# Output stage of a tiled pooling trunk: the inner form of product P2 from the second block on, with its weight sums made in place

## The chip, the cores and the metric

The kernel runs on one core of a Trainium2 chip. The metric is the device time of one execution in microseconds (us). It was run three times: 909.86, 910.41 and 911.19 us, median 910.41 us. One further execution was profiled; every view named below is of that one.

## What is computed

The layer is one pre-norm residual sub-layer and a final norm, over 4096 frames of 1024 channels, all in float32:

```python
u, gate = jnp.split(h @ in_w, 2, axis=-1)
pooled = jnp.stack([trailing_mean(ug[:, :, g], w) for g, w in enumerate((2, 4, 8, 16))], axis=2) - ug
mixed = jnp.einsum('bsgc,gcd->bsgd', pooled, group_w) + group_b
y = mixed.reshape(b, s, 1024) * scale * jax.nn.silu(gate)
out = rms_norm(x + y @ out_w, final_norm_w)
```

Here `h` is the normed input. The change is in the last line, the product `y @ out_w` with the residual and the final norm behind it, which is called the output stage below.

## The kernel before, in words

**Stages.** The kernel first forms weights, then multiplies the normed input by two halves of the widened projection (steps "a" and "b", four blocks of 1024 frames each), pools, and stores `y` to DRAM as `yd`. The output stage (steps "o") then takes eight blocks of 512 frames, numbered 0 to 7. Every step is one product of a seven-product Strassen-Winograd scheme, so each block of the output stage has seven steps, in the order P1, P7, P6, P2, P5, P4, P3 (`ORDER_OUT`).

**One product.** A block's `y` (512 frames x 1024 channels) is split in four quarters of 256 frames x 512 channels, `out_w` in four quarters of 512 x 512. Each product multiplies a sum of quarters of `y` by a sum of quarters of `out_w`. Every float32 operand is split into a high part (a copy on ScalarE, which rounds it) and a remainder (a subtraction on VectorE); `split` (line 167 and around) does this. A product of two split operands takes three passes: high by high, high by remainder, remainder by high (`mm3`, line 603). The split operand of `y` lies in one of four tiles `op0` to `op3`, taken in turn, and is TensorE's stationary operand in this stage; the split weights lie in tiles `w1` to `w7`, one pair for each product, for the whole stage. A plain product is two row groups x four k-tiles x three passes = 24 matmuls of 128 x 512.

**The inner form.** From block 2 on, P2 is not done plainly. Its own operands (256 x 512 by 512 x 512) are split in quarters again and multiplied by seven smaller products: 7 x two k-tiles x three passes = 42 matmuls of 128 x 256 (`product_inner`, line 701). Five of them are issued in the step of P2, one inside P5 and one behind it. `split_inner` makes four sums of the `y` operand's quarters (128 x 256 each, on VectorE) and splits the operand and the sums, so the step takes two op tiles. Three of the seven inner weights are quarters of the split weight tile `w2`, read as they are. The other four (P7, P6, P5, P4) are sums of quarters of the raw weight, `wod2` in DRAM. `form_inner` makes them once, in block 1: `load_inner` loads the two raw halves, stage 0 makes the four sums in two fresh tiles, stages 1 and 2 split two sums each into four tiles kept for the rest of the run (`kept`, tiles named `inner`).

**Tiles.** All else shares 19 tiles of 128 x 1024 floats: `st0` to `st10` and `vt0` to `vt7`. `take` pops the tile that has been free longest from one of two lists; `give` puts one back when the program text is done with it. The reuse is by program order: an instruction that writes a tile taken again waits until whatever used it last, a store's reading included, is over.

**Order.** `advance` loads four steps ahead and, in the output stage, splits two steps ahead (`split_reach`), so in the step of block 0's P3 the operand of block 1's P7 is formed and split. A scheduler then fixes one order of instructions for each engine. Engines run their own list in that order and wait for each other by semaphores.

**Behind a product.** `evict_o` moves the results from the PSUM banks: P1 to the banks of the sum on ScalarE, P7, P6 and P2 to residual rows `hs` on ScalarE, with `x` added by a GpSimd-issued transfer (`add_h`, line 884), P5, P4 and P3 by additions on VectorE (line 1067). After P4 and after P3, `finish` squares the 256 rows on ScalarE (line 943), takes the root, has four tiny GpSimd operations sharpen the reciprocal, scales the rows on VectorE (line 947), stores them to `out` (line 951) and gives their tiles back.

Of the kernel before, what the change touches and what calls it, by code (L numbers as in the profile page):

```python
# [10 lines left out]
F32 = mybir.dt.float32  # L11
F32R = mybir.dt.float32r
# [3 lines left out]
P = 128  # L16
D = 1024
S = 4096
H = 512
# [11 lines left out]
P1, P2, P3, P4, P5, P6, P7 = range(1, 8)  # L31
# [33 lines left out]
def kernel(  # L65
# [38 lines left out]
    mem = ctx.enter_context(tc.tile_pool(name="mem", bufs=1))  # L104
# [6 lines left out]
    def new_w(i):  # L111
        return [
            mem.tile([P, 2, 2, H], F32R, tag=f"w{i}_{h}", name=f"w{i}_{h}") for h in range(2)
        ]

    w = {i: new_w(i) for i in (P1, P2, P6, P7)}
    ops = [mem.tile([P, 4 * H], F32R, tag=f"op{i}", name=f"op{i}") for i in range(4)]
    sts = [mem.tile([P, D], F32, tag=f"st{i}", name=f"st{i}") for i in range(NS)]
    st = Slots(sts)

    def renew(t):
        i = next(i for i, u in enumerate(sts) if u is t)
        return mem.tile([P, D], F32R, tag=f"st{i}", name=f"inner{i}")

    st.renew = renew
    vt = Slots(
        [mem.tile([P, 2 * (HIST + H)], F32, tag=f"vt{i}", name=f"vt{i}") for i in range(NV)]
    )
# [11 lines left out]
    keep = [3]  # L140

    def take(pattern="p (a b) -> p a b", pool=None, **sizes):
        sizes = sizes or {"a": 2}
        if pool is None:
            spare = len(vt.free) > keep[0] or not st.free
            pool = vt if spare and vt.age() < st.age() else st
        return pool.take(lambda t: t[:, 0:D].rearrange(pattern, **sizes))
# [4 lines left out]
    def give(ap):  # L152
        next(p for p in (st, vt, early, early5) if id(ap) in p.used).give(ap)

    def add(dst, a, b):
        nc.vector.tensor_tensor(out=dst, in0=a, in1=b, op=ALU.add)  # L156

    def sub(dst, a, b):
        return nc.vector.tensor_tensor(out=dst, in0=a, in1=b, op=ALU.subtract)  # L159
# [4 lines left out]
    def copy(dst, src, func=AF.Copy):  # L164
        return nc.scalar.activation(dst, src, func)  # L165

    def split(dst, src):

        latest_copy[0] = copy(dst[:, 0], src).ins
        latest_split[0] = sub(dst[:, 1], src, dst[:, 0].bitcast(F32)).ins  # L170
# [104 lines left out]
    parts, t2 = {}, {}  # L275
# [157 lines left out]
    sums, held = {}, {}  # L433
# [25 lines left out]
    def store_rs(b, half, rs):  # L459
        nc.gpsimd.dma_start(out=rd[b][half][0].rearrange("(p j) -> p j", j=4), in_=rs)  # L460
# [41 lines left out]
    def next_op(pattern, **sizes):  # L502
        t = ops[turn[0] % 4]
        turn[0] += 1
        return t.rearrange(pattern, **sizes)
# [123 lines left out]

    inner, inner_w, kept = {}, {}, []

    def quarter(u, j):

        return u.rearrange("p k (s a) -> p k s a", s=2)[:, :, :, j * P : (j + 1) * P]

    def load_inner():
        inner_w["raw"] = [take() for _ in range(2)]
        for h, u in enumerate(inner_w["raw"]):  # L640
            nc.sync.dma_start(out=u, in_=wod[P2][h])

    def form_inner(stage):

        pattern, sizes = "p (n k s a) -> p n k s a", dict(n=2, k=2, s=2)
        if stage == 0:
            us = inner_w.pop("raw")
            b11, b12 = (quarter(us[0], j) for j in range(2))
            b21, b22 = (quarter(us[1], j) for j in range(2))
            raw = inner_w["sums"] = [take(pattern, **sizes) for _ in range(2)]  # L650
            (t3, t2), (t1, t4) = ([r[:, n] for n in range(2)] for r in raw)
            sub(t3, b22, b12)
            add(t2, t3, b11)
            sub(t1, b22, t2)
            sub(t4, b21, t2)
            for u in us:
                give(u)
            return
        r = inner_w["sums"][stage - 1]
        hi, lo = (kept.pop().rearrange(pattern, **sizes) for _ in range(2))  # L660
        copy(hi, r)
        sub(lo, r, hi.bitcast(F32))
        give(r)
        for n, i in enumerate(((P7, P6), (P5, P4))[stage - 1]):
            inner_w[i] = [v[:, n] for v in (hi, lo)]
        for i, (h, j) in {P1: (0, 0), P2: (1, 0), P3: (1, 1)}.items():
            inner_w[i] = [quarter(w[P2][h][:, s], j) for s in range(2)]

    def split_inner(u):

# [232 lines left out]

    def split_o(b, i):
        s = oxs[b]
        if i == P2 and b > 1:
            return split_inner(s["12"])
        t = next_op("p (s a b) -> p s a b", s=2, a=4)
        if i == P7:
            s["3"] = take("p (a b) -> p a b", a=4)  # L910
            sub(s["3"], s["11"], s["21"])
        elif i == P6:
            add(s["21"], s["21"], s["22"])
            sub(s["11"], s["21"], s["11"])
        elif i == P3:
            sub(s["12"], s["12"], s["11"])
            give(s.pop("11"))
        key = {P1: "11", P7: "3", P6: "11", P2: "12", P5: "21", P4: "22", P3: "12"}[i]
        split(t, s[key])
        if i not in (P1, P6, P2):  # L920
            give(s.pop(key))
        return t
# [329 lines left out]
    for n, (h, k) in enumerate(chunks):  # L1252
        o = fold(
            1, k, gw[1], ru[1, k], pairs_of[n], early5, n < 2, spread_first if n == 1 else None
        )
# [103 lines left out]
        )  # L1359

    scales, summed = {}, []
    stages = (P6, P5, P4)
    stages = (P6, P5, P4)

    for n in range(2, len(steps)):
        kind, b, i = steps[n]
        ahead = kind == "a" and b + 1 < NB
        keep[0] = 5 if kind == "b" and b == NB - 1 else 3
        advance("load", n, load, load_reach)
        if ahead:  # L1370
            rows, squares = row_plan(b)
            for half, rs in scales.items():
                store_rs(b + 1, half, rs)
                load_rstd(b + 1, half)
            scales.clear()
            for j in squares.get(i, ()):
                with tc.issue_after(latest_copy[0] if n == 3 else evicted[0]):
                    square_row(b + 1, j // 4, j % 4)
                if j % 4 == 3:
                    summed.append(j // 4)  # L1380
            for j in rows.get(i, ()):
                load_row(b + 1, j // 4, j % 4, early if b == 0 and i == P7 else None)
        if kind == "o" and b == 1 and len(kept) < 4 and not inner_w:
            while len(kept) < 4 and len(st.free) > 2:
                kept.append(st.keep())
            if len(kept) == 4:
                load_inner()
        elif kept:
            keep[0] = 0
        advance("split", n, split_step, split_reach)  # L1390
        if kind == "o" and b == 1 and i in stages:
            with tc.issue_after(latest_split[0]), tc.issue_after(latest_copy[0]):
                form_inner(stages.index(i))
        with tc.issue_after(latest_split[0]) if summed else nullcontext():
            for half in summed:
                scales[half] = stats(b + 1, half)
        summed.clear()
        if n == 2:
            with tc.issue_after(first_saves[0]):
                for place, u in stores:  # L1400
                    nc.gpsimd.dma_start(out=place, in_=u)
            for place, u in stores:
                if id(u) in early5.used:
                    give(u)
        with tc.issue_after(latest_split[0]):
            form(n + 2)
        if kind == "a" and b == 0:
            with tc.issue_after(latest_split[0]):
                rest_of_first(n)
        pool_due(n)  # L1410
        since = n - (NB - 1) * len(ORDER_IN) - 2
        if 0 <= since < len(ORDER_IN):
            form_wb(ORDER_IN[since])
        run(n)
        if kind == "a" and b == 2 and i == P7:
            save_t3()
        if 0 <= since < len(ORDER_IN):
            with tc.issue_after(evicted[0]):
                split_wb(ORDER_IN[since])
        if 0 <= since + 1 < len(ORDER_IN):  # L1420
            load_wb(ORDER_IN[since + 1])
        if kind in ("a", "b"):
            pool_later(n)
            if kind == "a":
                pool_due(n)
            if kind == "b" and b == NB - 1:
                load_w(wod, i)
            if kind == "b" and b in (1, 2) and i == P5:
                make_wo(b - 1)
            if kind == "b" and b == NB - 1 and i == P3:  # L1430
                f = take("p (a b) -> p a b", a=2)
                nc.sync.dma_start(
                    out=f.rearrange("p a b -> p (a b)"), in_=final_w.partition_broadcast(P)
                )
                fw.append(f)
# [52 lines left out]
```

## Time and profile before

| | us |
|---|---|
| median of 3 runs (lowest to highest) | 910.41 (909.86 to 911.19) |
| the profiled execution, whole | 910.49 |
| its span, first to last instruction | 908.7 |
| around the span | 1.79 |
| VectorE, ScalarE, GpSimd busy in the span | 715.5, 485.9, 84.6 |
| granted TensorE clock, mean | 0.999 |

The output stage fills the last third. TensorE's products of block 0 run from 614.87 to 651.13 us, those of block 1 from 651.13 to 687.39, and so on to block 7, behind whose products the last evictions and stores follow. Rows of the timeline give start, duration, engine, line, operation and tiles, and in brackets the idle time ahead with what ended it.

### The profile page before, as it was taken

The page shows a single profiled execution, that of the slowest core. Times are in us where ns is not written, and L with a number is a line of the kernel's source. Part 1 is how long each engine was busy: PE and PEld are TensorE (multiplying, and loading weights), DVE is VectorE, ACT ScalarE, POOL GpSimd, SP SyncE. Part 2 cuts the span into 40 slices and gives each one's busy share as a digit, 9 for nine tenths or more (in the row PEclk, how much of TensorE's full clock was granted, in tenths as well). Part 3 has the DMA queues.
Part 4 walks back from the last instruction along what each step waited for, and adds up shares of the span by engine and source line. Part 5 has one row for each costly group of instructions (what it writes and reads, how often), then busy time and mean ns, then how long its engine had stood idle before and what let it go on. Part 6 is the DMA issues. An engine that isn't in the chain of part 4 may idle for free.

```text
span 908.7 us, 11590 instructions
## 1 busy us (share of the span) xinstructions
PE 900.7 (99%) x4320; PEld 790.1 (87%) x4320; DVE 715.5 (79%) x843; ACT 485.9 (53%) x735; POOL 84.6 (9%) x166
## 2 busy tenths in 40 slices
PE   9999999999999999999999999999999999999997
PEld 7888888888888888888888888888888898988886
DVE  3889995985995997685786599599759768868686
ACT  7869547447446555355345445645545535445444
POOL 0020100100110000000000000001122113212200
PEclk9999999999999999999999999999999999999999
DMA  9987776577575454134616715618585675675732
GB/s 343 401 300 230 268 241 240 190 267 245 218 271 193 162 207 140 47 140 138 255 72 217 267 70 174 200 54 225 179 234 160 169 205 162 163 220 156 180 139 94
DMA packets 70841, 178.10 MB, mean 196 GB/s; under 512 B 6528, under 2 KB 24320, under 8 KB 70784
## 3 DMA queue, kind: packets, MB, share of 16 engines
q1 hardware_dynamic: 58160, 144.82, 46.0%
q0 software_dynamic: 11904, 31.48, 13.3%
q10 hardware_dynamic: 720, 1.06, 0.3%
q8 instruction: 34, 0.56, 0.3%
q14 instruction: 23, 0.19, 0.1%
HBM read 116.50 MB, written 60.83 MB: 195 GB/s over the span
## 4 chain that ended last, share of the span: by engine, by line
PE 95%; DVE 2%; DMA 1%; ACT 1%; issue 0%; DVEq 0%; ACTq 0%; SPq 0%
PE bank L603 89%; PE bank L701 3%; PE bank L406 3%; DMA st<-wvd 1%; DMA t3d<-st 0%; DMA early<-in_group_w 0%; DVE vt L1067 0%; DVE st L159 0%; ACT st L974 0%; ACT st L446 0%; DVE vt L162 0%; PE bank L472 0%; DVE op L159 0%; DVE vt L1026 0%; DVE st L156 0%
## 5 line engine op out<-in xcount | busy, mean ns | idle before, releaser
L603 PE MATMUL bank<-op,w 128*128 128x512 f32 x2688 | 581.2, 379 | 0.2 <-ACT st L165 0.2
L603 PEld LDWEIGHTS bank<-op,w 128*128 128x128 f32 x2688 | 507.8, 189 | 72.9 <-ACT st L165 0.6
L603 PE MATMUL bank<-w,op 128*128 128x512 f32 (+1 forms) x1212 | 262.2, 377 | 0.0
L603 PEld LDWEIGHTS bank<-w,op 128*128 128x128 f32 x1212 | 226.0, 189 | 31.0
L159 DVE TENSOR_TENSOR op<-st,op 128x1024 fp32r<-128x1024 f32 x129 | 156.5, 1220 | 76.4 <-ACT op L165 76.0
L165 ACT ACTIVATE op<-st 128x1024 fp32r<-128x1024 f32 x129 | 134.7, 1052 | 123.3 <-PE bank L603 82.6
L165 ACT ACTIVATE vt<-bank 128x512 f32<-128x512 f32 x105 | 61.4, 593 | 44.7 <-PE bank L603 44.2
L159 DVE TENSOR_TENSOR op<-vt,op 128x1024 fp32r<-128x1024 f32 x43 | 52.4, 1220 | 20.8 <-ACT op L165 20.6
L165 ACT ACTIVATE op<-vt 128x1024 fp32r<-128x1024 f32 x43 | 45.0, 1052 | 28.9 <-PE bank L603 24.9
L165 ACT ACTIVATE st<-bank 128x512 f32<-128x512 f32 x67 | 39.0, 592 | 38.0 <-PE bank L603 26.1
L884 POOL DMA_DIRECT2D st<-in_x x19 | 16.9, 894 | 387.7 <-DVE op L159 354.1
L159 DVE TENSOR_TENSOR st<-st,st 128x1024 f32<-128x1024 f32 (+1 forms) x43 | 46.7, 1108 | 3.2 <-ACT st L943 1.3
L165 ACT ACTIVATE bank<-bank 128x512 f32<-128x512 f32 x48 | 27.9, 581 | 35.6 <-PE bank L603 35.4
L755 DVE TENSOR_TENSOR_SCAN vt<-vt,window 128x1040 f32<-128x1040 f32 x16 | 38.1, 2379 | 2.8 <-ACT vt L165 2.7
L159 DVE TENSOR_TENSOR w<-st,w 128x1024 fp32r<-128x1024 f32 x25 | 30.2, 1220 | 11.7 <-ACT w L165 11.7
L165 ACT ACTIVATE w<-st 128x1024 fp32r<-128x1024 f32 x25 | 26.0, 1052 | 16.3 <-PE bank L603 10.8
L806 DVE SCALAR_TENSOR_TENSOR st<-vt,colt,st 128x512 f32<-128x512 f32 x46 | 32.4, 746 | 1.7 <-ACT st L165 1.6
L165 ACT ACTIVATE st<-st 128x1024 f32<-128x1024 f32 x16 | 16.9, 1058 | 29.9 <-DVE st L156 29.7
L801 DVE SCALAR_TENSOR_TENSOR vt<-vt,vt 128x1024 f32<-128x1024 f32 x24 | 29.3, 1221 | 0.3
L947 DVE SCALAR_TENSOR_TENSOR vt<-vt,ors,st 128x1024 f32<-128x1024 f32 x18 | 22.5, 1282 | 8.0 <-POOL ors L225 8.0
L162 DVE TENSOR_TENSOR st<-st,vt 128x1024 f32<-128x1024 f32 x22 | 26.1, 1216 | 2.1 <-DMA vt<-rd 2.1
L1067 DVE TENSOR_TENSOR st<-bank,st 128x512 f32<-128x512 f32 x23 | 15.8, 689 | 13.8 <-PE bank L603 13.7
(136 smaller groups left out, 661.6 us busy)
## 6 DMA issues: line engine op xcount, KB each, us to landing
st<-in_xt SPq DMA_DIRECT2D x28, 512.0 KB, 5.9
sd<-st POOLq DMA_DIRECT2D x28, 512.0 KB, 4.3
st<-sd SPq DMA_DIRECT2D x24, 512.0 KB, 4.4
yd<-st SPq DMA_DIRECT2D x23, 512.0 KB, 2.6
st<-in_x SPq DMA_DIRECT2D x20, 512.0 KB, 6.3
st<-yd SPq DMA_DIRECT2D x20, 512.0 KB, 4.7
out<-vt SPq DMA_DIRECT2D x18, 512.0 KB, 4.5
st<-wod SPq DMA_DIRECT2D x15, 512.0 KB, 3.4
```

Source lines behind the costliest of these rows:

```text
L159: return nc.vector.tensor_tensor(out=dst, in0=a, in1=b, op=ALU.subtract)
L162: nc.vector.tensor_tensor(out=dst, in0=a, in1=b, op=ALU.mult)
L165: return nc.scalar.activation(dst, src, func)
L406: latest[0] = nc.tensor.matmul(ps, a[:, kk, 2 * j + t, :], maps, start=t + m == 0, stop=t == 1 and m == len(pairs) - 1,).ins
L603: latest[0] = nc.tensor.matmul(ps, a, b, start=start and n == 0, stop=stop and n == 2, skip_group_check=True).ins
L701: latest[0] = nc.tensor.matmul(ps, x1, x2, start=i in (P1, P7) and k + n == 0, stop=k == 1 and n == 2, skip_group_check=True,).ins
L755: nc.vector.tensor_tensor_scan(out=sums_[:, HIST:], data0=flat[:, HIST:], data1=flat[:, HIST - win : 2 * end - win], initial=first_sum, op ...
L801: nc.vector.scalar_tensor_tensor(out=s[:, :, at : at + H], in0=s[:, :, at : at + H], scalar=1.0 / win, in1=v[:, :, HIST:], op0=ALU.mult, o ...
L806: nc.vector.scalar_tensor_tensor(out=sg[:, j], in0=s[:, j, at : at + H], scalar=bias_c[2 * grp + j], in1=sg[:, j], op0=ALU.add, op1=ALU.mult,)
L884: nc.gpsimd.dma_start(out=hs[b][half, j][:, n], in_=x[row_of(b, half, j), n * H : (n + 1) * H], accum_op=ALU.add,)
L947: nc.vector.scalar_tensor_tensor(out=us[j], in0=us[j], scalar=rs[:, j : j + 1], in1=fw[0], op0=ALU.mult, op1=ALU.mult,)
L1067: partial["added"] = nc.vector.tensor_tensor(out=dst, in0=src, in1=dst, op=ALU.add).ins
```

## The change

The inner form is used from block 1 on. What it needs is therefore formed in block 0. `load_inner` moves to the step of block 0's P2, the sums to P5, the splits to P4 (weights P7 and P6) and P3 (weights P5 and P4). The four sums are made in place, in the two raw tiles themselves, and each weight is split by itself, a 128 x 512 copy and a 128 x 512 subtraction. The split weight P5 goes into the quarter of `w2` that only a plain P2 reads; so three kept tiles do instead of four, each holding one weight's high part and remainder. The kept tiles are now collected from the first step of the output stage on, as soon as more than three of the 19 are free, and the two raw tiles are held until the last split.

```diff
-        return mem.tile([P, D], F32R, tag=f"st{i}", name=f"inner{i}")
+        return mem.tile([P, 2, H], F32R, tag=f"st{i}", name=f"inner{i}")
...
-    def form_inner(stage):
...
+    def sum_inner():
+        us = raw["held"]
+        t1, t3 = (quarter(us[0], j) for j in range(2))
+        t4, t2 = (quarter(us[1], j) for j in range(2))
+        sub(t1, t3, t1)
+        sub(t3, t2, t3)
+        sub(t2, t2, t1)
+        sub(t4, t4, t2)
+        raw.update({P5: t1, P6: t2, P7: t3, P4: t4})
+        for p, (h, j) in {P1: (0, 0), P2: (1, 0), P3: (1, 1)}.items():
+            inner_w[p] = [quarter(w[P2][h][:, s], j) for s in range(2)]
+
+    def split_weight(p):
+        if p == P5:
+            home = [quarter(w[P2][0][:, s], 1) for s in range(2)]
+        else:
+            t = kept.pop().rearrange("p k (h s a) -> p h k s a", h=2, s=2)
+            home = [t[:, s] for s in range(2)]
+        copy(home[0], raw[p])
+        sub(home[1], raw[p], home[0].bitcast(F32))
+        inner_w[p] = home
+
+    def end_weights():
+        for u in raw.pop("held"):
+            give(u)
...
-        if i == P2 and b > 1:
+        if i == P2 and b > 0:
             return split_inner(s["12"])
...
+    forming = {
+        (0, P2): load_inner,
+        (0, P5): sum_inner,
+        (0, P4): lambda: (split_weight(P7), split_weight(P6)),
+        (0, P3): lambda: (split_weight(P5), split_weight(P4), end_weights()),
+    }
...
-        if kind == "o" and b == 1 and len(kept) < 4 and not inner_w:
-            while len(kept) < 4 and len(st.free) > 2:
-                kept.append(st.keep())
-            if len(kept) == 4:
-                load_inner()
-        elif kept:
-            keep[0] = 0
+        if kind == "o":
+            while len(gathered) < 3 and st.free and len(st.free) + len(vt.free) > 3:
+                gathered.append(st.keep())
+                kept.append(gathered[-1])
+            if b > 0:
+                keep[0] = 0
...
-        if kind == "o" and b == 1 and i in stages:
+        if kind == "o" and (b, i) in forming:
             with tc.issue_after(latest_split[0]), tc.issue_after(latest_copy[0]):
-                form_inner(stages.index(i))
+                forming[b, i]()
```

More of the change, by code (lines that the diff above doesn't have):

```diff
@@ L628, in product_in @@
             between[8]()
-    inner, inner_w, kept = {}, {}, []
+    inner, inner_w, kept, gathered = {}, {}, [], []
     def quarter(u, j):
         return u.rearrange("p k (s a) -> p k s a", s=2)[:, :, :, j * P : (j + 1) * P]
+    raw = {}
     def load_inner():
-        inner_w["raw"] = [take() for _ in range(2)]
-        for h, u in enumerate(inner_w["raw"]):
+        raw["held"] = [take() for _ in range(2)]
+        for h, u in enumerate(raw["held"]):
             nc.sync.dma_start(out=u, in_=wod[P2][h])
-    def form_inner(stage):
[L645 to L667, printed above, removed]
@@ L1361 @@
     scales, summed = {}, []
-    stages = (P6, P5, P4)
-    stages = (P6, P5, P4)
+    forming = {
[4 more added lines that the diff above has]
+    }
     for n in range(2, len(steps)):
```

## The prediction

> **What bounds the kernel now.** I read the page first, then the chain that ended last, then who waited, then the stretches block by block.
>
> ```profile
> PE 900.7 (99%) x4320; PEld 790.1 (87%) x4320; DVE 715.5 (79%) x843; ACT 485.9 (53%) x735; POOL 84.6 (9%) x166
> ```
> ```profile
> 599.98 102.95 PE bank L603 x477
> 702.93 3.35 PE bank L701 x30
> 706.28 2.59 PE bank L603 x12
> 708.87 0.67 PE bank L701 x6
> 709.54 2.59 PE bank L603 x12
> 712.13 0.67 PE bank L701 x6
> 712.80 25.90 PE bank L603 x120
> ```
> ```profile
> PE bank L603 <- ACT st L165: 0.2, 1, 0.2
> ```
> ```profile
> 614.87:651.13 36.26, 36.26 (x169) 31.75 (x169) 31.42 (x33) 19.99 (x29) 6.28 (x11) 1.00 0.76 210
> 651.13:687.39 36.26, 36.26 (x169) 31.75 (x169) 24.71 (x28) 16.30 (x25) 8.64 (x16) 1.00 0.70 197
> ```
>
> TensorE is busy in 99% of the span, and the chain through the output stage is matmuls end to end. The third fence holds the only wait of its products that the profile gives, 0.2 us, long before this stage. The last fence holds blocks 0 and 1 (length, then TensorE's busy time): neither has an idle moment, and the chain has none in block 2. So a matmul less is time saved, and any wait of TensorE is time lost in full, since nothing later has slack to pay it back. VectorE is busy 31.4 of 36.3 us in block 0, the block that is to take on more.
>
> **What the change saves.** Line 701 is the inner form: in block 2, 30 + 6 + 6 = 42 matmuls in 3.35 + 0.67 + 0.67 = 4.69 us, 111.7 ns each. A plain product is 24 of the 120 in 25.90 us, 5.18 us. One block more saves 5.18 - 4.69 = **0.49 us**. That is 0.05% of the time. The Trainium skill (TensorE: Matmul & The Clock Gate, "Wait — 56ns, not 53.3ns?") puts warm matmuls N ÷ 2.4 GHz + 2.5 ns apart; for 256 columns that is an estimate of 109.2 ns, and the saving by it would be 0.59 us. The row has 111.7 ns, so the measurement decides.
>
> **What it adds and moves.** Two 512 KB loads of the raw weight, four sums (4 x 128x512), four copies and four remainders (128x512) move into block 0 and early block 1; the sums and remainders were about 5 us of VectorE in block 1. Block 1 gains what every inner block has: four 128x256 sums, one more operand split (a copy and a remainder of 128x1024) and six short additions. None of that is TensorE's. It costs nothing while TensorE's next operand is there in time. So I followed the queues of the changed program, with these rows as durations (start, duration; blocks 0 and 1):
>
> ```profile
> 628.44 0.33 SPq L810 DMA_DIRECT2D yd<-vt  x1
> ...
> 642.93 0.32 SPq L641 DMA_DIRECT2D vt<-wod  x1
> 652.26 1.53 SPq L951 DMA_DIRECT2D out<-st  x2
> ```
> ```profile
> vt<-yd SPq DMA_DIRECT2D x5, 512.0 KB, 5.5
> ...
> st<-wod SPq DMA_DIRECT2D x3, 512.0 KB, 3.3
> ...
> yd<-vt SPq DMA_DIRECT2D x1, 512.0 KB, 5.1
> ```
> ```profile
> 631.84 1.20 DVE L159 TENSOR_TENSOR op<-st,op 128x1024 fp32r<-128x1024 f32 x1
> ...
> 650.95 2.48 DVE L947 SCALAR_TENSOR_TENSOR st<-st,ors,st 128x1024 f32<-128x1024 f32 x2 [1.22 <-POOL ors L225]
> 653.35 0.68 DVE L1067 TENSOR_TENSOR vt<-bank,vt 128x512 f32<-128x512 f32 x1
> 653.95 1.21 DVE L159 TENSOR_TENSOR op<-st,op 128x1024 fp32r<-128x1024 f32 x1
> 655.20 1.23 DVE L159 TENSOR_TENSOR st<-st,vt 128x1024 f32<-128x1024 f32 x1
> 656.34 0.15 DVE L210 RECIPROCAL ors<-otmp 128x2 f32<-128x2 f32 x1
> 657.71 1.28 DVE L947 SCALAR_TENSOR_TENSOR st<-st,ors,st 128x1024 f32<-128x1024 f32 x1 [1.22 <-POOL ors L225]
> ...
> 661.24 0.69 DVE L159 TENSOR_TENSOR vt<-vt,st 128x512 f32<-128x512 f32 x1
> 661.96 0.69 DVE L156 TENSOR_TENSOR vt<-vt,st 128x512 f32<-128x512 f32 x1
> ...
> 691.12 0.42 DVE L159 TENSOR_TENSOR st<-vt 128x256 f32<-128x256 f32 x1
> ```
> ```profile
> 654.06 1.07 ACT L943 ACTIVATE vt<-vt 128x1024 f32<-128x1024 f32 x1 [2.06 <-DVE vt L1067]
> 655.03 0.18 ACT L943 ACTIVATION_READ_ACCUMULATOR vt<-vt 128x1 f32 x1
> ...
> 655.64 0.27 ACT L206 ACTIVATE otmp<-oss,eps 128x2 f32<-128x2 f32 x1
> 656.13 1.06 ACT L165 ACTIVATE op<-st 128x1024 fp32r<-128x1024 f32 x1 [0.22 <-PE bank L603]
> ```
>
> Three things are read from them. Starts of independent neighbours lie closer than the durations: 1.13 us for a 128x1024 VectorE operation (655.20 to 656.34), 1.20 for line 947, 0.66 and 0.34 for 128x512 and 128x256, 0.97 for a ScalarE copy (654.06 to 655.03). An operation that needs its predecessor starts 0.03 us behind its end (661.24 + 0.69 to 661.96). And a copy that waits for a product starts 0.18 us before the product's modelled end (656.13 against 651.13 + 5.18 = 656.31).
>
> *Block 0.* The second raw load goes into `st0`, which must first be read by the split at 631.84. In the changed program that split ends near 633.2, and ahead of the load in SyncE's queue stands a load of `y` whose tile must first be stored: 628.44 + 5.1 = 633.5. So the load is issued at about 633.9 and lands 3.3 to 5.5 us later, 637.2 to 639.4. Behind it VectorE does four dependent sums (4 x 0.72), a remainder for P1 (1.13) and two weight remainders (2 x 0.66): it comes to the additions of P5 at 642.5 to 644.7. P3 needs the first of them by P4's end, 651.13 - 5.18 = 645.95, so that is hidden, with 0.5 us to spare at worst. But P4's additions, its squares, its root and the scaling at 650.95 then come 0 to 0.7 us late.
>
> *First wait, before P7 of block 1.* Before, the difference that P7 multiplies was formed well ahead in a free tile. Now five tiles are held, none is free, and the difference is written into `st1`: a row tile of block 0 that line 947 has just scaled and that is on its way to `out`. The built program has the difference waiting for that store, and in VectorE's queue behind the scaling, P2's first operand and the reciprocal of the other half. The store is issued at 652.26. All the stores to `out` together:
>
> ```profile
> DMA to landing us min/median/max: 1.8/3.0/7.9
> ```
>
> By the median it lands at 655.3, before VectorE is free. So VectorE sets the time: root 655.64 + 0.27, reciprocal to 656.1, difference 656.1 to 657.3. Copy on ScalarE to 658.4; on VectorE line 947 (657.71) comes first, so the remainder runs 658.9 to 660.1. TensorE ends P1 at 656.31, does 9 inner matmuls (1.0 us) and waits from 657.3 for the copy: 1.1 us. Four matmuls and three inner ones (1.2 us) later it waits for the remainder: 0.5 us. In all 1.6 us, and 2.3 if block 0 comes 0.7 us late. I take **2.0 us**. Queued behind the waiting difference are the scaling of the other half, the remainders of weights P5 and P4, and the operands of P5 and P6.
>
> *Second wait, between P7 and P6 of block 1.* ScalarE's order in the changed program is:
>
> ```
> op0 <- st1    (P7's operand)
> w2, inner10   (weights P5 and P4)
> bank3, st9    (evictions)
> op0 <- vt5    (P5's operand: op0 is free when P7 has been multiplied)
> op1 <- vt3    (P6's operand)
> op3 <- st1    (the four inner sums)
> ```
>
> P6 comes next on TensorE, but its copy stands behind a copy that waits for the end of P7; call that end E. P5's copy runs from E - 0.18, P6's is done at E + 1.85, that of `op3` at E + 3.0. VectorE, held up above, began P7's remainder at 658.9, which is E - 5.55 (1.23 to its end, then 20 matmuls, 4.32). Behind it stand two weight remainders (2 x 0.66), line 947 (1.20) and P5's sum, which ends at E - 0.7; P6's difference ends at E + 0.8, the last of the four inner sums at E + 1.9, and the three remainders at E + 3.05, 4.2 and 5.3. TensorE has six inner matmuls in hand (to E + 0.67), waits 1.2 us for P6's copy, does four matmuls (0.86), waits 0.3 for `op3`, does four inner ones (0.45), and waits 0.7 for P6's remainder. That is **2.2 us**. The rest of block 1 has its operands in time: P5's remainder was made in the same run, and P4's copy is ready a whole product ahead. From block 2 on three tiles are held instead of four, and the matmuls stand in the old order.
>
> **Sum.** -0.49 + 2.0 + 2.2 = +3.7 us on the profiled execution's 910.49 (span 908.7, 1.79 around it): 914.2. The median of the runs is 0.08 lower: **914.1 us**, 0.4% slower.
>
> **Rivals.**
>
> *No wait.* The first wait vanishes if the copy of P7's operand ends by 657.3, so if the difference starts by 655.0; the second if P6's copy is done at E + 0.67. Then only the saving stays: 910.41 - 0.49 = 909.9. For it speaks that 31.4 us of VectorE in block 0 hid the old order wholly. Against it: the operand and reciprocal ahead of the difference end at 655.16 and 656.1 before anything is added, and no speed brings P6's copy ahead of one that waits for P7. Chance 0.05.
>
> *Only the copies are late.* If the remainders keep up, 1.1 + 1.2 us is left: 910.41 - 0.49 + 2.3 = 912.2. Speaks for it that the remainder terms hang on longer chains. Chance 0.08, half of it under the bound for slower.
>
> *The store or the raw load is late too.* With the longest landing of the row above, 7.9 us, the store at 652.3 lands at 660.2 and the difference starts 4.1 us later than I have it: 914.1 + 4.1 = 918.2. A raw load that lands after 639.9 makes P3 wait in block 0 as well, us for us. In the changed program two loads stand right ahead of the store in SyncE's queue; before, its last issue was at 642.93. Chance 0.10. The Trainium skill (TensorE: Matmul & The Clock Gate, "Part 1: The HAM clock gate") says that the clock halves after an idle window of about 3.4 us; only this case would have such a gap, no run here shows one, and as an estimate a window at half rate would add 1.7 us.
>
> **How the numbers follow.** The forecast has 0.77. Its range: 912.1 where both waits shrink to the copies; above, 914.1 + 1.3 for a store 1.3 us later, plus up to five restarts of TensorE that each may show a weight load no longer hidden:
>
> ```profile
> L603 PEld LDWEIGHTS bank<-w,op 128*128 128x128 f32 x1212 | 226.0, 189 | 31.0
> ```
>
> That row's mean is 189 ns; five restarts are 0.9 us. That gives 912.1 to 916.3. Left out are the case without a wait, most of the dearer one and half of the cheaper, under 2 in 10. A measurement of this kernel tells about 0.2% (1.8 us) from no change, so slower means above 912.2: 0.77 + 0.10 + 0.04 = 0.91. The saving alone is inside the bound: of the case without a wait 0.04 goes to same, with the other 0.04 that is 0.08, and 0.01 to faster, should it save more than the rows show.
>
> **What would show it.** Right: idle time of line 603 in block 1 alone, about 2 us before P7 and 2 us before P6, released by ScalarE's or VectorE's writing of an op tile; the difference on VectorE after 656, in a tile just stored; 4338 matmuls instead of 4320; blocks 2 to 7 at 35.77 us. Wrong: block 1 at 35.8 us without idle time, or idle time in block 0 or after block 1.

## The result, and the profile after

The changed kernel took 919.02 us (median of five runs, 918.46 to 921.15), the kernel before beside it 910.16. The ratio is 1.0104, 95% interval 1.0088 to 1.012. The forecast was 914.1 with a range of 912.1 to 916.3: the direction was right, the size was not. The execution profiled after took 918.46 us (span 916.7), 7.97 more than the one before. Two of the five runs took 921 us with a mean granted clock of 0.994 in place of 0.996 to 0.997; the account below is that of the profiled one.

First the page: TensorE's row.

```profile
PE 903.2 (99%) x4338; PEld 791.7 (86%) x4338; DVE 722.0 (79%) x856; ACT 487.0 (53%) x738; POOL 79.2 (9%) x166
```

There are 4338 matmuls instead of 4320, as forecast, but they are busy 2.5 us longer, where the saving should have made them 0.5 us shorter. So something made matmuls slower. The rest of the 8 us is idle time, and the view of TensorE's waits (us in all, times, longest) says whose:

```profile
PE bank L603 <- DVE st L1071: 2.3, 1, 2.3
PE bank L603 <- ACT op L165: 2.1, 2, 1.3
PE bank L603 <- DVE op L159: 1.0, 2, 0.8
```

The last two rows are the forecast's two waits, each with one wait for a copy and one for a remainder. The first row isn't in the forecast. TensorE's timeline shows where the waits lie. First before, then after:

```profile
614.71 88.22 PE L603 MATMUL bank<-w,op 128*128 128x512 f32 x408
702.77 0.50 PE L701 MATMUL bank<-w,op 128*128 128x256 f32 x3
```
```profile
639.83 6.21 PE L603 MATMUL bank<-w,op 128*128 128x512 f32 x28
648.33 12.20 PE L603 MATMUL bank<-w,op 128*128 128x512 f32 x48 [2.30 <-DVE st L1071]
660.37 1.17 PE L705 MATMUL bank<-w,op 128*128 128x256 f32 x9
662.35 1.13 PE L603 MATMUL bank<-w,op 128*128 128x512 f32 x4 [0.82 <-ACT op L165]
663.32 0.50 PE L705 MATMUL bank<-w,op 128*128 128x256 f32 x3
664.61 4.58 PE L603 MATMUL bank<-w,op 128*128 128x512 f32 x20 [0.79 <-DVE op L159]
669.03 0.83 PE L705 MATMUL bank<-inner,op 128*128 128x256 f32 x6
671.12 1.13 PE L603 MATMUL bank<-w,op 128*128 128x512 f32 x4 [1.26 <-ACT op L165]
672.09 0.47 PE L705 MATMUL bank<-w,op 128*128 128x256 f32 x2
672.39 0.39 PE L705 MATMUL bank<-inner,op 128*128 128x256 f32 x2
673.02 4.58 PE L603 MATMUL bank<-w,op 128*128 128x512 f32 x20 [0.24 <-DVE op L159]
```

Before, 408 matmuls run from block 0's first to block 2's inner form without a break: 88.06 us, 0.2158 each. After, I take the distances between starts and subtract what the matmuls between them take (0.2158 and 0.1117 us):

- Ahead of P3 of block 0: 648.33 - 639.83 - 28 x 0.2158 = **2.46 us** (2.30 idle, the rest restart).
- The 48 matmuls behind that gap: 660.37 - 648.33 - 48 x 0.2158 = **1.68 us**, without a pause.
- Around P7 of block 1: 664.61 - 660.37 less 4 long and 12 short matmuls = **2.04 us** (forecast 2.0).
- Around P6: 673.02 - 664.61 less 24 long and 10 short = **2.11 us** (forecast 2.2), and 0.10 us behind it.

With the 0.49 us saved and a start that was 0.08 later this gives 2.46 + 1.68 + 2.04 + 2.11 + 0.10 - 0.49 + 0.08 = 7.98 us, the whole difference. So the forecast lacks the first two terms, 4.1 us, both in block 0.

The chain of waits shows where they come from (start, duration, what), as SyncE's queue, VectorE's timeline and the view of landings (KB each, us from issue to landing) do:

```profile
634.11 7.92 DMA st<-wod
642.07 0.40 issue
642.47 0.70 DVE st L159
...
648.33 4.45 PE bank L603 x12
```
```profile
633.64 0.37 SPq L871 DMA_DIRECT2D vt<-yd  x1
634.11 0.64 SPq L643 DMA_DIRECT2D st<-wod  x1
```
```profile
642.47 0.69 DVE L159 TENSOR_TENSOR st<-st 128x512 f32<-128x512 f32 x1 [6.63 <-DMA st<-wod]
...
647.59 2.47 DVE L1071 TENSOR_TENSOR st<-bank,st 128x512 f32<-128x512 f32 x4
```
```profile
vt<-yd SPq DMA_DIRECT2D x1, 512.0 KB, 5.7
st<-wod SPq DMA_DIRECT2D x1, 512.0 KB, 7.9
```

The second raw load was issued at 634.1, 0.2 us later than forecast, but took 7.9 us instead of 3.3 to 5.5. VectorE stood 6.63 us with the in-place sum at the head of its queue. P5's additions, behind that sum, came at 647.6, and P3 needs the bank that the first of them empties.

The second term is the clock. The view of stretches has TensorE's busy time in its second figure and the granted clock in the third from the right:

```profile
643.00:646.00 3.00, 3.00 (x15) 2.31 (x13) 2.90 (x5) 1.26 (x2) 0.00 (x0) 1.00 0.34 72
646.00:649.00 3.00, 0.70 (x3) 0.58 (x3) 3.00 (x6) 0.00 (x0) 0.00 (x0) 0.86 0.00 0
649.00:653.00 4.00, 4.00 (x14) 3.29 (x13) 1.26 (x3) 3.43 (x5) 0.18 (x1) 0.68 0.06 16
653.00:656.00 3.00, 3.00 (x15) 2.62 (x15) 1.78 (x4) 2.31 (x5) 0.78 (x4) 1.00 0.25 82
```

At the end of the gap it falls: 3 x 0.14 + 4 x 0.32 = 1.70 us of full clock are missing. The clock's record has one stretch at half here, 3413 ns, which costs half of that, 1.71 us. (It has another as the run ends, as in the kernel before.)

### The profile page after: what moved, and what is told of

It reads as the page before. It is cut to its first block, busy times and chain, and to the rows that moved or that the text cites. A ratio compares the mean times of both kernels' runs of the same rounds, so it can differ in the third digit from the quotient of the medians.

```text
span 916.7 us, 11659 instructions
## 1 busy us (share of the span) xinstructions
PE 903.2 (99%) x4338; PEld 791.7 (86%) x4338; DVE 722.0 (79%) x856; ACT 487.0 (53%) x738; POOL 79.2 (9%) x166
## 4 chain that ended last, share of the span: by engine, by line
PE 87%; DVE 7%; DMA 2%; issue 2%; ACT 1%; POOL 0%; DVEq 0%; ACTq 0%; POOLq 0%; SPq 0%
PE bank L603 80%; PE bank L705 3%; PE bank L406 3%; DVE op L159 1%; DVE st L159 1%; DMA st<-wod 1%; DVE vt L759 1%; DMA st<-wvd 1%; DVE w L159 1%; DVE st L156 1%; DMA t3d<-st 0%; DMA early<-in_group_w 0%; DVE vt L156 0%; DVE st L810 0%; ACT vt L978 0%
## 5 line engine op out<-in xcount | busy, mean ns | idle before, releaser
L159 DVE TENSOR_TENSOR op<-st,op 128x1024 fp32r<-128x1024 f32 x119 | 144.4, 1219 | 66.1 <-ACT op L165 65.7
L165 ACT ACTIVATE op<-st 128x1024 fp32r<-128x1024 f32 x119 | 124.2, 1052 | 97.9 <-PE bank L603 60.1
L159 DVE TENSOR_TENSOR op<-vt,op 128x1024 fp32r<-128x1024 f32 x54 | 65.6, 1220 | 33.3 <-ACT op L165 33.1
L165 ACT ACTIVATE op<-vt 128x1024 fp32r<-128x1024 f32 x54 | 56.3, 1052 | 53.4 <-PE bank L603 45.4
L165 ACT ACTIVATE vt<-bank 128x512 f32<-128x512 f32 x97 | 56.6, 593 | 39.7 <-PE bank L603 39.2
L888 POOL DMA_DIRECT2D st<-in_x x27 | 24.3, 899 | 433.7 <-DVE op L159 354.2
L159 DVE TENSOR_TENSOR w<-st,w 128x1024 fp32r<-128x1024 f32 (+1 forms) x26 | 30.8, 1198 | 11.7 <-ACT w L165 11.7
L165 ACT ACTIVATE w<-st 128x1024 fp32r<-128x1024 f32 (+1 forms) x26 | 26.6, 1034 | 16.4 <-PE bank L603 10.8
L1071 DVE TENSOR_TENSOR st<-bank,st 128x512 f32<-128x512 f32 (+1 forms) x34 | 22.6, 671 | 9.5 <-PE bank L603 9.4
L951 DVE SCALAR_TENSOR_TENSOR st<-st,ors,st 128x1024 f32<-128x1024 f32 x16 | 20.2, 1283 | 6.7 <-POOL ors L225 6.7
```

The lines of the kernel that those rows point to most:

```text
L888: nc.gpsimd.dma_start(out=hs[b][half, j][:, n], in_=x[row_of(b, half, j), n * H : (n + 1) * H], accum_op=ALU.add,)
L951: nc.vector.scalar_tensor_tensor(out=us[j], in0=us[j], scalar=rs[:, j : j + 1], in1=fw[0], op0=ALU.mult, op1=ALU.mult,)
L1071: partial["added"] = nc.vector.tensor_tensor(out=dst, in0=src, in1=dst, op=ALU.add).ins
```

## The experiments

The theory (A) after this: two independent faults. In block 0 the operation on VectorE that waits for the transfer issued at 634 us holds up P5's additions, and the gap draws a stretch at half clock. In block 1 P7's difference is written into a tile that is being stored, though other tiles are free. The rivals stand with each expectation. All kernels are the changed one with the edit shown.

### Both raw loads early

```diff
+        keep[0], was = 1, keep[0]
         raw["held"] = [take() for _ in range(2)]
+        keep[0] = was
```

`take` leaves `keep[0]` = 3 tiles of the `vt` list untouched. With 1 here both loads go into `vt` tiles that are free earlier, and both are issued by 621 us.

> Against the changed kernel (919.0 us) only the tiles of the two raw weight loads differ: both go into vt tiles that are free early, so the second load no longer stands behind the split that frees st0 and behind the store of a y tile. Theory A (the late second load alone makes VectorE late for the additions of P5, P3 of block 0 waits 2.3 us for them, and the granted clock falls behind that wait, 1.7 us): both terms go, 919.0 - 4.0 = 915.0 us, no clock below 1.00 in block 0, and the two waits of block 1 stay near 2 us each. Theory B (VectorE's added sums and remainders are what is too much for block 0, wherever the load lands): a wait of 1 us or more before P3 stays, 917 us or above.

Measured: 913.94 us, ratio 1.0038 (1.0024 to 1.0052). TensorE's timeline has no gap in block 0, and block 1 has the waits of the changed kernel:

```profile
657.78 1.13 PE L603 MATMUL bank<-w,op 128*128 128x512 f32 x4 [1.04 <-ACT op L165]
...
660.03 4.58 PE L603 MATMUL bank<-w,op 128*128 128x512 f32 x20 [0.79 <-DVE op L159]
...
666.55 1.13 PE L603 MATMUL bank<-w,op 128*128 128x512 f32 x4 [1.26 <-ACT op L165]
...
668.44 4.58 PE L603 MATMUL bank<-w,op 128*128 128x512 f32 x20 [0.23 <-DVE op L159]
```

The granted clock is 1.00 through all of it (mean 0.999), though block 1's waits add up to 3.3 us: the half clock belongs to the long gap. This is the time that was forecast, 914.1. From block 0's first matmul to block 2's inner form it is 92.04 us (614.13 to 706.17), 3.98 more than before where the forecast has 3.7: with the load in time, the sum of the remaining terms holds to 0.3 us.

### The reserve lifted

```diff
-            if b > 0:
+            if b > 0 or i in (P4, P3):
                 keep[0] = 0
```

> Against the changed kernel only the reserve of three vt tiles is dropped from the step of block 0's P4 on, so that the difference for P7 of block 1 takes a free vt tile and not the row tile st1 that is being stored. Theory A (the reserve, not a lack of tiles, made the difference late, and all that stands behind it in VectorE's and ScalarE's queues): both waits of block 1 go, 4.4 us with the restarts, the waits before P3 of block 0 and the low clock stay: 919.0 - 4.4 = 914.6 us. Theory B (VectorE has too much to do around the start of block 1 for P7 and P6 to be in time in any tile): at least one of the waits before P7 and P6 stays, 917 us or above.

Measured: 913.97 us, 1.0037 (1.0024 to 1.0051). Block 1's four waits are gone and block 0's gap stays:

```profile
648.25 22.67 PE L603 MATMUL bank<-w,op 128*128 128x512 f32 x96 [2.71 <-DVE st L1071]
670.76 1.50 PE L705 MATMUL bank<-w,op 128*128 128x256 f32 x12
```

The 96 matmuls take 22.51 us to the next start instead of 20.72: again 1.79 us for one stretch at half clock. So the tile for P7's difference wasn't forced on the program by a lack of tiles, but by a reserve.

### Both together

> Both edits together. Theory A: no wait of TensorE in blocks 0 and 1, the clock at 1.00, and only the saving of one inner product is left, 910.16 - 0.49 = 909.7 us, ratio 0.9995. Theory B (the added work costs something wherever it is put): a wait of 0.5 us or more in block 0 or 1, 910.2 us or above, ratio 1.000 or more.

Measured: 915.92 us, 1.0067 (1.0054 to 1.0079), a miss by 6 us. VectorE's and TensorE's rows show why:

```profile
643.20 1.23 DVE L159 TENSOR_TENSOR vt<-vt,st 128x1024 f32<-128x1024 f32 x1 [6.42 <-DMA st<-yd]
```
```profile
649.88 22.67 PE L603 MATMUL bank<-w,op 128*128 128x512 f32 x96 [3.52 <-DVE st L1073]
```

The raw load is no longer late, but a load of `y` into an `st` tile now takes its place in SyncE's queue, and P7's difference, which reads it, has moved ahead of P5's additions. Theory A has to be put more widely: any VectorE operation ahead of those additions that waits for the transfer issued at 634 us stops P3.

### The gap filled with matmuls

```diff
+            if (b, i) == (0, P3):
+                a = split_up[n]
+                for c in range(11):
+                    nc.tensor.matmul(
+                        sets["spare"][0], a[:, 0, c % 4, 0:P], w[P3][0][:, 0, c % 2],
+                        start=True, stop=True, skip_group_check=True,
+                    )
```

> The changed kernel with 11 matmuls of 128x512 more, into a bank that is free then, between P4 and P3 of block 0, where TensorE waits 2.3 us; 11 x 0.216 = 2.4 us. They compute nothing that is used. Theory A (the fall of the granted clock to one half for 3.4 us comes from the idle gap): no gap, no low clock, 919.0 - 1.7 + 0.1 = 917.4 us, faster with more work. Theory B (the slow matmuls behind the gap have another cause, such as data that comes late or the queue starting again): the 12 matmuls behind still take 4.4 us in place of 2.6, 919.1 us.

Measured: 919.72 us, 1.0105 (1.009 to 1.0121).

```profile
645.74 2.69 PE L1155 MATMUL bank<-w,op 128*128 128x512 f32 x11
648.38 10.63 PE L603 MATMUL bank<-w,op 128*128 128x512 f32 x48
662.06 0.70 PE L603 MATMUL bank<-w,op 128*128 128x512 f32 x2 [3.05 <-ACT op L165]
```

Behind the filled gap the 48 matmuls take 10.63 us instead of 12.20, at a granted clock of 1.00 (649 to 659 us). But the scheduler no longer pulls inner matmuls ahead in block 1, the first gap there grows to 3.05 us, and the one stretch at half clock now comes behind that one and a second gap of 0.84 us, from about 664.1 us on. As a comparison of times it misses, since block 1 changed with it; for the clock it shows that the stretch goes with the gap.

### The waits gone, and the price of an inner product

`waits_gone` is both edits together, and P7's difference issued behind P5's additions:

```diff
+            with tc.issue_after(partial["added"]) if b == 1 else nullcontext():
+                sub(s["3"], s["11"], s["21"])
```

`from_block_two` is the same with `b > 1` for the inner form. Its plain P2 of block 1 reads the quarter of the weight that the kept sum has replaced, so it multiplies by other numbers in the same time.

> The two earlier mends together (both raw loads early into the next two places; the reserve of three places lifted from block 0's last steps on), and P7's difference in block 1 issued only behind P5's additions of block 0, so that no VectorE operation ahead of those additions waits for the transfer that is issued at about 634 us. Theory A (what cost time is an operation on VectorE, ahead of P5's additions, that waits for that transfer, the half clock that follows the gap, and the two waits of block 1): all are gone, only the saving of 0.49 us is left: before less 0.5, about 909.9 us, a granted clock near 1.00, no gap of TensorE over 0.5 us between 640 and 690 us. Rival B (the late transfer stalls TensorE whichever way it is ordered, since DMA traffic of block 0 itself is what is late): a gap of over 2 us stays somewhere in blocks 0 or 1, 912 us or more.

> As waits_gone, but the inner form of P2 is used from the third block on, as in the kernel before, so that only the early making of the weight sums in the raw tiles is left of the change. Theory A (the inner form of one product saves 42 products of 111.7 ns against 24 plain ones, 0.49 us; the making of the sums costs nothing where nothing waits): the time of the kernel before, within 0.2 us of 910.4, and 0.5 us above waits_gone. Rival B (the inner form saves nothing in a block whose neighbours keep TensorE full, as its products are limited by something else): equal to waits_gone.

Measured: 909.92 us, 0.9997 (0.9989 to 1.0006), and 910.19 us, 1.0001 (0.9992 to 1.001). The waits are gone, and theory A holds in its wider form. From block 0's first matmul to block 2's inner form `from_block_two` takes 88.05 us, the kernel before 88.06: forming the weights early costs nothing once nothing waits. But `waits_gone` takes 88.01, where 87.57 was expected. The saving is missing, and one row of its timeline shows a small wait in the inner form of block 1:

```profile
667.27 0.71 PE L707 MATMUL bank<-w,op 128*128 128x256 f32 x4 [0.17 <-DVE op L159]
```

With what is lost around it (12 inner matmuls from 666.04 to 667.82 instead of in 1.34 us) it takes 0.44 us.

### The last wait

`waits_gone`, with P5's operand of block 1 split behind the inner operands:

```diff
-        split(t, s[key])
+        with tc.issue_after(latest_split[0]) if (b, i) == (1, P5) else nullcontext():
+            split(t, s[key])
```

> waits_gone, with P5's operand of block 1 split behind the remainders of the inner operands. In waits_gone's trace the inner matmuls of block 1 waited 0.17 us for such a remainder and lost 0.27 us more around it, so that of the saving of 0.49 us only 0.05 was left. Theory A (VectorE had P5's remainder ahead of the one that was needed): block 1 runs without a gap, its products take 35.77 us instead of 36.26, the time is 909.8, 0.4 us below waits_gone's trace for the same start. Rival B (the inner products of block 1 are late for another reason): the gap stays and block 1 takes 36.2 us.

Measured: 909.65 us, 0.9992 (0.9983 to 1.0001). Blocks 1 and 2 in the view of stretches:

```profile
651.21:686.98 35.77, 35.77 (x188) 31.91 (x187) 31.89 (x43) 20.10 (x31) 10.22 (x20) 1.00 0.76 199
686.98:722.75 35.77, 35.77 (x188) 31.91 (x187) 26.00 (x32) 17.73 (x27) 8.20 (x16) 1.00 0.69 184
```

Block 1 is now as full as block 2, and the distance is 87.57 us (614.79 to 702.36): 0.49 us less than before, the forecast's saving to the hundredth. In the time of the whole it is within what can't be told from no change.

### Why the load took 7.9 us

Two kernels: one without the accumulating transfers of block 0 (`add_h` not called), one with the second raw load issued from ScalarE's queue.

> The changed kernel without the accumulating transfers of block 0 (the addition of x to that block's output rows is left out). Theory A (the raw load issued at 634 us took 7.9 us because GpSimd's accumulating transfers shared the DMA engines): it lands in 5.5 us or less, by 639.6, the gap ahead of P3 in block 0 falls from 2.30 to under 0.3 us and with it the half clock; block 1's waits stay: about 915 us. Rival B (it is late by its place in SyncE's queue behind the loads ahead of it): it lands 7 us or more after its issue, and the time stays at about 919 us.

> The changed kernel with the second raw load issued from ScalarE's queue in the place of SyncE's. Theory A (the DMA engines themselves are shared with GpSimd's accumulating transfers): a transfer on a queue of its own still takes 6 us or more, the gap ahead of P3 stays over 0.8 us, 916 to 919 us. Rival B (it waits behind the loads ahead of it in SyncE's queue): it lands within about 4 us of its issue, no gap ahead of P3, about 915 us.

Measured: 914.2 us and 914.12 us, both 1.0047 (1.0033 to 1.0061), both without a gap in block 0 and with block 1's waits. The landings of the two loads, first without the additions, then on ScalarE's queue:

```profile
vt<-yd SPq DMA_DIRECT2D x1, 512.0 KB, 3.6
st<-wod SPq DMA_DIRECT2D x1, 512.0 KB, 4.6
```
```profile
st<-wod ACTq DMA_DIRECT2D x1, 512.0 KB, 3.4
vt<-yd SPq DMA_DIRECT2D x1, 512.0 KB, 6.8
```

Each mends block 0 alone, but neither is a clean test. On ScalarE's queue the load waits for its tile ahead of ScalarE's evictions, and those release GpSimd's transfers:

```profile
632.87 0.33 ACTq L643 DMA_DIRECT2D st<-wod  x1
633.24 0.60 ACT L165 ACTIVATE st<-bank 128x512 f32<-128x512 f32 x1 [7.12 <-DVE op L159]
```

ScalarE stood for 7.12 us, GpSimd issued nothing between 626.55 and 634.26 us, and from the load's issue to its landing none of the DMA engines' time went to GpSimd's packets. So its 3.4 us does not refute A. Without the additions, the load of `y` ahead was issued 2.3 us before the raw load (630.58 and 632.87) in place of 0.5 us, so 4.6 us does not refute a wait behind that load either; only B's own figure, 7 us or more, fails. In both experiments the raw load was also issued 1.2 us earlier (632.87). With 7.9 us it would still have landed 0.9 us too late, by the point of 639.9 that the forecast had.

The traces settle more than the times do. From the issue of the raw load to its landing, GpSimd's queue had 42% of the DMA engines' time in the changed kernel: 3.3 of the 7.9 us. The 4.6 us that are left are what the load took without the additions. As an estimate, then, GpSimd's transfers cost about 3.3 us, and the place behind the load of `y` about 1.3 of the rest, since a raw load alone in quiet stretches takes 3.2 to 3.3 us. In `raw_early` a load of `y` holds the same place behind the same load, with 41% for GpSimd's queue, and took 8.4 us: the place is slow, whatever is loaded in it. No run changes the spacing of the two loads alone.

### P6's operand ahead

The raw loads early, and the splits of weights P5 and P4 one step later:

```diff
-        (0, P3): lambda: (split_weight(P5), split_weight(P4), end_weights()),
+        (1, P1): lambda: (split_weight(P5), split_weight(P4), end_weights()),
```

> raw_early with the splits of the weights P5 and P4 moved one step later (from block 0's P3 to block 1's P1). By that P7's difference still goes into the row tile that is being stored, but on VectorE it stands ahead of the reciprocal, and P6's difference stands right behind it, ahead of the two weight remainders and the second half's scaling; on ScalarE P6's copy stands ahead of P5's. Theory A (the second wait is made by what the queues hold ahead of P6's difference and copy; the first by the reciprocal and the scaling ahead of P7's difference and remainder): the second wait is gone and the first falls from 1.83 to about 0.5 us; 910.5 to 911.5 us. Rival B (the wait is for the store of the row tile, which is as late as before): the first wait stays near 1.8 us; 912 us or more.

Measured: 920.16 us, 1.0096 (1.0077 to 1.0114), a miss of 9 us. The four runs took 916.71 to 924.40 us, and the trace is that of the last. The waits of TensorE in it:

```profile
PE bank L603 <- DVE st L1073: 4.4, 1, 4.4
PE bank L707 <- DVE st L717: 3.3, 1, 3.3
...
PE bank L603 <- ACT op L165: 0.4, 1, 0.4
```

Around P7 0.4 us is left of 1.83, around P6 nothing. That agrees with theory A, though with block 0's end as much later it is no clean test. But the edit also changed which tile is taken when. The four sums of the inner operand of block 1 now stand at the head of VectorE's queue and wait for a load of `y` that lands at 641.7, so the gap of block 0 is back, with 4.4 us. A load read further on made another of 3.3 us. At each the clock's record has 6827 ns at half, two stretches of 3413.

## Why the prediction went wrong, point by point

- **The saving** (0.49 us) was right: 87.57 against 88.06 us where nothing waits.
- **Block 0** is the step that failed: the landing "3.3 to 5.5 us later", by which the wait was "hidden, with 0.5 us to spare at worst". It was 7.9 us. The text gives 639.9 as the point from which P3 waits "us for us"; the load landed at 642.0, 2.1 us past it, and TensorE lost 2.46. The mechanism and the point were there, as part of a rival with a chance of 0.10, but without a time for the raw load. That the rival's 918.2 lies near the measured 919.0 is chance: it was the price of a late store, and the difference that was to wait for the store began 0.03 us behind the reciprocal. The landings were taken from loads as they stood in the kernel before. There, a load also issued 0.4 us behind another (622.22 us) took 5.5 us, but GpSimd's queue had only 18% of the DMA engines' time during it; the raw load met 42%. The same prediction quotes a row with landings up to 7.9 us.
- **The clock** was weighed and set aside. Its price, 1.7 us, was right (1.68). The Trainium skill (TensorE: Matmul & The Clock Gate, "Part 1: The HAM clock gate") gives an idle window of about 3.4 us and says that the windows run freely. The length of the stretch agrees (3413 ns). The gap that drew it was 2.30 us, shorter than the window that the page names for the idle state, so the forecast's reading, that only a gap of that size counts, was wrong here.
- **The first wait** was right in mechanism and size, 2.04 for 2.0 us, the size in part by luck. The difference ran right behind the reciprocal of the other half (659.78 and 659.98) and the scaling came ahead of the remainder, as worked out. But the 1.6 us worked out was raised to 2.0 for a late block 0, and the excess is there in `raw_early` too, where block 0 is in time. It came from the remainder: it started 3.35 us behind the difference (663.33) in place of 2.8. GpSimd's four operations ahead of the scaling ended 2.3 us behind the start of the reciprocal (662.10), where the kernel before has 1.3. The reason given for the tile was wrong: tiles were free, and `take` held three back. `reserve_lifted` shows it.
- **The second wait** was right in size: 2.11 for 2.2 us. P5's and P6's copies stand in the order given (669.06, two in 2.00 us). In parts it was 1.42, 0.19 and 0.51 us for the copy, `op3` and the remainder, where the forecast has 1.2, 0.3 and 0.7. In `reserve_lifted` one edit takes both waits away, so both hang on the late difference; which of copy and difference held P6 longer is not separated.
- **The rivals.** "No wait" is what `no_last_wait` reached, at 909.65, with four edits that the change doesn't have. "Only the copies are late" did not come: 1.0 of the 3.1 us of idle time in block 1 was waited for remainders.

## What to carry to other kernels

Where an engine's queue is in program order, ask of every operation ahead of an urgent one what transfer it waits for, and price that transfer by the slowest landing amid the traffic it will meet, not by a row with less of it. A gap on TensorE as long as those that drew half clock here, 2.30 us or more, should carry the price of such a stretch, 1.7 us, in the sum and not in a side remark. And moving one load or one use may only hand its late place to another: after each edit the same slot in the queue has to be looked at again.

## What the hardware showed that was not expected

- Gaps of TensorE of 2.30, 2.71, 3.05 and 3.52 us each drew one stretch of 3413 ns at half clock, those of 4.41 and 3.32 us two. Gaps of 0.2 to 1.3 us, four within 12 us and 3.3 us in all, drew none. (Behind the one of 3.05 us came a second gap of 0.84 us before the clock fell.) No run has a gap between 1.3 and 2.3 us, so where the limit lies is not known.
- A 512 KB load took 7.9 us in SyncE's queue 0.5 us behind another load and beside GpSimd's accumulating transfers; GpSimd's queue had 42% of the DMA engines' time during it. It took 4.6 us without those transfers and 2.3 us behind the other load, and 3.4 us on ScalarE's queue, where its own wait had put the transfers off. That load, waiting for its tile, had ScalarE stand for 7.12 us.
